# Last bank of a down projection summed in two column halves, and the final norm's gain multiplied in before the rows' factor

## The chip, the cores and the metric

The kernel runs on one core of one Trainium2 chip. The metric is the time of one execution in device microseconds; three runs of the kernel before give 1261.11, 1261.15 and 1261.88 us, a median of 1261.15 us.

The engines are named as the profile names them: PE multiplies matrices and PEld loads its weights, DVE is the vector engine, ACT the scalar engine, POOL the general-purpose engine, SP the queue that issues nearly all transfers. Each works through its own queue in the order written.

## What is computed

One decoder layer on 256 tokens of width 2048: three kinds of self-attention, a cross-attention to a memory, and a gated feed-forward block with 5632 inner columns, each added to x. At the end stands a root-mean-square norm over each token's 2048 values. The change touches only the last two lines:

```python
x = x + conv_glu_ffn(rms_norm(x, g_ffn[l]), w_up[l], conv_w[l], conv_b[l], w_down[l])
return rms_norm(x, g_final)

def rms_norm(x, g):
    y = x * rsqrt(mean(x * x, axis=-1) + NORM_EPS)
    return y * g
```

Everything is float32.

## The kernel before

The tokens are two groups of 128, t = 0 and t = 1. The weights stream through PE in pieces of 128 x 2048 floats; every piece is split by ACT into a high part `hi` (L141) and by DVE into the rest `lo` (L148), and three matmuls (high x high, high x low, low x high) make one float32 product. A list by hand, `before(i, ...)` and `after(i, ...)`, sets where the other work stands between the pieces; no scheduler moves anything, so the order of the code is the order on each engine.

The down projection takes 44 pieces, k = 0 to 43, of 128 rows of `w_down` each. Its result is 256 tokens by 2048 columns: for each t four blocks of 512 columns, n = 0 to 3, each in a PSUM bank of its own, so all eight banks are held (`outs[t, n]`). The first 42 pieces are multiplied into all banks in turn. The last two pieces (`TAIL = 2`) are held back, and then finished bank by bank: for t = 0 the banks n = 0 to 3, then for t = 1 the same, six matmuls of 512 columns each (`down_mm`, L852 to L854).

As soon as a bank is complete, its share of the final norm follows:

- DVE adds the bank to the residual x (L891), which lies in SBUF as `xT`.
- ACT squares the sum and adds up each token's squares into one column of `ss` (`square_sum`, L266); a small ACT instruction, ACTIVATION_READ_ACCUMULATOR, hands the sum out.
- DVE multiplies some blocks by the final gain `gfin` into the output tile `og` (L899); `og` takes a buffer of the pool `raw` and carries that name in the profile.
- After the fourth bank three small DVE instructions (L900 to L902) make mean square plus epsilon, and POOL raises it to the power -0.5 (L904): the factor `r` of each token.
- `finish(n, t, og, r)` scales a block by r and issues its transfer to `out` from SP (L867). For t = 0 the four blocks have their gain already, and are scaled by ACT (n = 0 and 1), DVE (n = 2) and POOL (n = 3) while t = 1 is being computed; DVE's part stands between two adds of t = 1. For t = 1 the blocks 0 and 2 have their gain in `og` and are scaled by ACT; the blocks 1 and 3 take gain and factor in one DVE instruction (L862).

The small sums for t = 1 (L900, over the first three columns of `ss`) stand behind the last add on DVE.

## Time and profile before

| | |
|---|---|
| median of three runs | 1261.15 us |
| the profiled execution's own time | 1260.96 us |
| its span, first to last instruction | 1259.2 us |
| PE busy | 1243.1 us, 99% of the span |
| DVE busy | 831.4 us, 66% |
| ACT busy | 630.3 us, 50% |
| POOL busy | 12.2 us |
| last matmul begins | 1249.80 us after the span's start |
| factor of t = 1 begins on POOL | 1252.14 us |
| last four output transfers are issued from | 1253.49 us |

The profile is one execution of the program on the chip. A line of its timeline gives the start in us from the span's start, the duration, the engine, the line of the kernel, the operation, output and inputs with their shapes, and in square brackets how long the engine had been idle before it and what released it. A DVE instruction may start up to 0.1 us before the one ahead of it ends, since they are pipelined.

### The profile page before, as it was taken

What the parts mean: (1) busy time and instruction counts of PE and PEld (TensorE: products, weight loads), DVE (VectorE), ACT (ScalarE), POOL (GpSimd) and SP (SyncE); (2) the same over time, 40 slices, a digit from 0 to 9 for tenths busy, and PEclk for the clock granted to TensorE, in tenths of its full rate; (3) what the DMA queues carried; (4) which work ended last, traced back from release to release, by engine and by line L of the source; (5) the groups of instructions that cost most, each with busy time, mean ns of one, the idle gap of its engine ahead of it and who ended that gap; (6) DMA issues with size and microseconds to landing.
All of it is one profiled execution on the core that took longest, in us unless ns stands there. A gap on an engine that the chain in (4) does not pass through costs nothing.

```text
span 1259.2 us, 17608 instructions
## 1 busy us (share of the span) xinstructions
PE 1243.1 (99%) x6928; PEld 1078.2 (86%) x6928; DVE 831.4 (66%) x1350; ACT 630.3 (50%) x979; POOL 12.2 (1%) x22
## 2 busy tenths in 40 slices
PE   7999999999999999999999999999999999999997
PEld 6888888988888899888888888888888888888885
DVE  5755677566568877776667768767676754544555
ACT  6545555556455656545444444444444544444444
POOL 0000000000000000000000000000000000000000
PEclk9999999999999999999999999999999999999999
DMA  8755554554566544565565565555656555555541
GB/s 301 236 176 188 186 167 162 181 183 159 174 223 215 170 167 162 202 203 171 167 200 182 186 197 174 183 199 184 198 170 201 186 183 200 181 187 200 175 160 67
DMA packets 104835, 233.23 MB, mean 185 GB/s; under 512 B 4336, under 2 KB 14896, under 8 KB 98992
## 3 DMA queue, kind: packets, MB, share of 16 engines
q1 hardware_dynamic: 104576, 232.05, 55.2%
q8 instruction: 54, 0.88, 0.3%
q14 instruction: 29, 0.24, 0.1%
q10 hardware_dynamic: 144, 0.03, 0.0%
q0 software_dynamic: 32, 0.02, 0.0%
HBM read 229.97 MB, written 2.12 MB: 184 GB/s over the span
## 4 chain that ended last, share of the span: by engine, by line
issue 58%; PE 39%; DMA 2%; DVE 0%; POOL 0%; ACT 0%; SPq 0%; DVEq 0%; POOLq 0%; ACTq 0%
PE acc L296 16%; PE acc L303 9%; PE acc L342 3%; PE acc L344 3%; PE acc L343 3%; DMA raw<-in_w_in 2%; PE at L402 1%; PE acc L299 1%; PE acc L298 1%; PE at L421 0%; PE at L445 0%; PE at L473 0%; PE at L474 0%; ACT hi L141 0%; POOL raw L866 0%
## 5 line engine op out<-in xcount | busy, mean ns | idle before, releaser
L148 DVE TENSOR_TENSOR lo<-raw,hi 128x1024 fp32r<-128x1024 f32 x423 | 517.1, 1223 | 368.1 <-ACT hi L141 367.5
L141 ACT CAST hi<-raw 128x1024 fp32r<-128x1024 f32 x423 | 442.9, 1048 | 480.6 <-PE acc L296 281.0
L296 PE MATMUL acc<-hT,hi 128*128 128x512 f32 x1776 | 631.3, 396 | 4.7 <-ACT hi L141 4.7
L303 PE MATMUL acc<-hT,lo 128*128 128x256 f32 x1840 | 517.7, 283 | 0.9 <-DVE lo L148 0.9
L296 PEld LDWEIGHTS acc<-hT,hi 128*128 128x128 f32 x1776 | 334.0, 188 | 82.0 <-ACT hi L141 5.3
L303 PEld LDWEIGHTS acc<-hT,lo 128*128 128x128 f32 x1840 | 345.6, 188 | 1.6 <-DVE lo L148 1.3
L296 PE MATMUL at<-hT,hi 128*128 128x512 f32 x528 | 189.6, 394 | 0.0
L303 PE MATMUL at<-hT,lo 128*128 128x256 f32 x528 | 149.3, 283 | 0.0
L296 PEld LDWEIGHTS at<-hT,hi 128*128 128x128 f32 x528 | 99.2, 188 | 22.8
L303 PEld LDWEIGHTS at<-hT,lo 128*128 128x128 f32 x528 | 99.3, 188 | 0.0
L854 PE MATMUL acc<-hi,al 128*128 128x512 f32 x220 | 86.8, 395 | 0.0
L853 PE MATMUL acc<-lo,ah 128*128 128x512 f32 x220 | 86.8, 395 | 0.0
L852 PE MATMUL acc<-hi,ah 128*128 128x512 f32 x220 | 86.8, 395 | 0.0
L342 PE MATMUL acc<-hi,hT 128*128 128x256 f32 (+1 forms) x224 | 74.8, 334 | 0.0
L344 PE MATMUL acc<-hi,hT 128*128 128x256 f32 (+1 forms) x224 | 74.0, 330 | 0.0
L343 PE MATMUL acc<-lo,hT 128*128 128x256 f32 (+1 forms) x224 | 73.9, 330 | 0.0
L852 PE MATMUL at<-hi,ah 128*128 128x512 f32 x132 | 52.1, 395 | 0.0
L854 PE MATMUL at<-hi,al 128*128 128x512 f32 x132 | 52.1, 395 | 0.0
L853 PE MATMUL at<-lo,ah 128*128 128x512 f32 x132 | 52.1, 394 | 0.0
L789 ACT ACTIVATE y<-y 128x256 f32<-128x256 f32 x44 | 18.4, 419 | 66.4 <-DVE y L785 66.4
L852 PEld LDWEIGHTS acc<-hi,ah 128*128 128x128 f32 x220 | 41.5, 188 | 9.7
L853 PEld LDWEIGHTS acc<-lo,ah 128*128 128x128 f32 x220 | 41.5, 188 | 9.7
(157 smaller groups left out, 1004.2 us busy)
## 6 DMA issues: line engine op xcount, KB each, us to landing
raw<-in_w_up SPq DMA_DIRECT2D x88, 1024.0 KB, 5.1
raw<-in_w_in SPq DMA_DIRECT2D x45, 1024.0 KB, 5.3
raw<-in_w_down SPq DMA_DIRECT2D x44, 1024.0 KB, 4.9
raw<-in_w_out SPq DMA_DIRECT2D x12, 1024.0 KB, 5.3
raw<-in_w_ckv SPq DMA_DIRECT2D x8, 1024.0 KB, 5.6
raw<-in_w_out SPq DMA_DIRECT2D x8, 512.0 KB, 5.0
raw<-in_w_cq SPq DMA_DIRECT2D x4, 1024.0 KB, 5.4
raw<-in_w_co SPq DMA_DIRECT2D x4, 1024.0 KB, 5.3
```

Of the source, the lines that this page charges most:

```text
L141: ACT.copy(hi, p.raw[:, h * HALF:(h + 1) * HALF])
L148: DVE.tensor_tensor(lo, p.raw[:, h * HALF:(h + 1) * HALF], hi.bitcast(F32), op=ALU.subtract)
L296: PE.matmul(accs[n], w, x, start=(i == 0), stop=False)
L298: PE.matmul(accs[n][:, :S], w, x[:, :S], start=(i == 0), stop=False)
L303: PE.matmul(accs[n][:, :S], lo[:, j, n * P:(n + 1) * P], src()[:, korder[i], :S], start=False, stop=(i == len(korder) - 1))
L342: PE.matmul(o, xh, hi[:, j, :], start=(i == 0), stop=False)
L343: PE.matmul(o, xh, lo[:, j, :], start=False, stop=False)
L344: PE.matmul(o, xl, hi[:, j, :], start=False, stop=(i == len(korder) - 1))
L789: after(cur[0] + 1 + n, lambda: ACT.activation(gate[k], gate[k], AF.Silu))
L852: PE.matmul(o, ah, wh, start=(k == 0), stop=False)
L853: PE.matmul(o, ah, wl, start=False, stop=False)
L854: PE.matmul(o, al, wh, start=False, stop=(k == KF - 1))
```

## The change

Only the end of the down projection, `finish` and the size of `ss3` are edited.

- For t = 1 the bank n = 3 is finished in two halves. The last two pieces are first multiplied into columns 0 to 255 of the bank, with six matmuls of 256 columns; then into columns 256 to 511, with six more, but into a bank of their own (`own`), which is started afresh and holds only the last two pieces' part. When the first half is done, DVE adds the whole bank, 512 columns, to x (its right half still lacks the last two pieces), and when the second is done, 256 columns of `own`.
- The squares of t = 1 come in five columns, the last two of 256 values each. The small sums over the first four (L896, L897) stand on DVE ahead of the add of the second half; only the last small instruction (L912) is behind it.
- Each block of t = 1 is multiplied by the gain as soon as it is added, as for t = 0, so DVE has four such multiplications for t = 1 (the last in two halves) where it had two.
- The scalings by r are dealt out anew. t = 0: ACT has n = 0 and 1, POOL n = 2 and 3, DVE none; they are issued in the order 2, 0, 3, 1. t = 1: DVE has n = 0 and 2, now a plain multiplication by r, ACT n = 1 and 3.
- `ss3` has 10 columns for 8.

```diff
-    def down_mm(p, k, h, t, n):
+    def down_mm(p, k, h, t, n, c0=0, c1=512, own=None):
         hi, lo = p.parts[h]
         ah, al = (a[:, t * P:(t + 1) * P] for a in parts[k])
-        o = outs[t, 2 * h + n]
-        wh, wl = hi[:, n * 512:(n + 1) * 512], lo[:, n * 512:(n + 1) * 512]
-        PE.matmul(o, ah, wh, start=(k == 0), stop=False)
+        o, first = (outs[t, 2 * h + n][:, c0:c1], 0) if own is None else (own, KF - TAIL)
+        wh, wl = (a[:, n * 512 + c0:n * 512 + c1] for a in (hi, lo))
+        PE.matmul(o, ah, wh, start=(k == first), stop=False)
...
     def finish(n, t, og, r):
         col = slice(n * 512, (n + 1) * 512)
-        if t and n % 2:
-            DVE.scalar_tensor_tensor(og[:, col], xtok(t, n), r, gfin["t"][:, col], op0=ALU.mult, op1=ALU.mult)
-        elif t or n < 2:
+        if t:
+            if n % 2:
+                ACT.activation(og[:, col], og[:, col], AF.Copy, scale=r)
+            else:
+                DVE.tensor_scalar_mul(og[:, col], og[:, col], r)
+        elif n < 2:
             ACT.activation(og[:, col], og[:, col], AF.Copy, scale=r)
         else:
-            (DVE, POOL)[n - 2].tensor_scalar_mul(og[:, col], og[:, col], r)
+            POOL.tensor_scalar_mul(og[:, col], og[:, col], r)
...
-                    ss = ss3[:, 4 * t:4 * t + 4]
-                    for n in range(4):
+                    ss = ss3[:, 5 * t:5 * t + 5]
+
+                    parts_of = ((0, 0, 512), (1, 0, 512), (2, 0, 512)) + (((3, 0, 256), (3, 256, 512)) if t else ((3, 0, 512),))
+                    for i, (n, c0, c1) in enumerate(parts_of):
+                        own = any_tile()[:, :c1 - c0] if c0 else None
                         for kk in range(KF - TAIL, KF):
-                            down_mm(fin[kk], kk, n // 2, t, n % 2)
-                        col = slice(n * 512, (n + 1) * 512)
-                        xc = xtok(t, n)
-                        DVE.tensor_tensor(xc, outs[t, n], xc, op=ALU.add)
-                        square_sum(xc, ss[:, n:n + 1])
+                            down_mm(fin[kk], kk, n // 2, t, n % 2, c0, c1, own)
+                        if t and i == len(parts_of) - 1:
+                            DVE.reduce_sum(ms[:, 0:1], ss[:, :i], axis=AX.X)
+                            DVE.tensor_scalar(ms[:, 0:1], ms[:, 0:1], 1.0 / D, EPS, op0=ALU.mult, op1=ALU.add)
+                        xc = xtok(t, n)[:, c0:c1]
+                        if own is None:
+                            DVE.tensor_tensor(xtok(t, n), outs[t, n], xtok(t, n), op=ALU.add)
+                        else:
+                            DVE.tensor_tensor(xc, own, xc, op=ALU.add)
+                        square_sum(xc, ss[:, i:i + 1], c1 - c0)
                         if done:
-                            for m in ((3, 0, 1), (2,), (), ())[n]:
+                            for m in ((2, 0), (3, 1), (), (), ())[i]:
                                 finish(m, *done)
-                        gains = ((), (0,), (), (2,)) if t else ((0,), (1,), (2,), (3,))
-                        for m in gains[n]:
-                            col = slice(m * 512, (m + 1) * 512)
-                            DVE.tensor_tensor(og[:, col], xtok(t, m), gfin["t"][:, col], op=ALU.mult)
-                    DVE.reduce_sum(ms[:, 0:1], ss[:, :3], axis=AX.X)
-                    DVE.tensor_scalar(ms[:, 0:1], ms[:, 0:1], 1.0 / D, EPS, op0=ALU.mult, op1=ALU.add)
-                    DVE.scalar_tensor_tensor(ms[:, 1:2], ss[:, 3:4], 1.0 / D, ms[:, 0:1], op0=ALU.mult, op1=ALU.add)
+                        col = slice(n * 512 + c0, n * 512 + c1)
+                        DVE.tensor_tensor(og[:, col], xc, gfin["t"][:, col], op=ALU.mult)
+                    if not t:
+                        DVE.reduce_sum(ms[:, 0:1], ss[:, :3], axis=AX.X)
+                        DVE.tensor_scalar(ms[:, 0:1], ms[:, 0:1], 1.0 / D, EPS, op0=ALU.mult, op1=ALU.add)
+                    DVE.scalar_tensor_tensor(ms[:, 1:2], ss[:, i:i + 1], 1.0 / D, ms[:, 0:1], op0=ALU.mult, op1=ALU.add)
```

This is how DVE's queue ends in the kernel before, from the first add of t = 1 on (`xT` is x, `raw` the output tile, `msf` and `ss_96` the small sums; the bracket names the engine whose count is waited for):

```order
L891 TENSOR_TENSOR xT<-at,xT 128x512 [waits PE_49] x2
L866 TENSOR_SCALAR raw<-raw,rfin 128x512 [waits Pool_49]
L899 TENSOR_TENSOR raw<-xT,gfin 128x512 [waits DVE_49]
L891 TENSOR_TENSOR xT<-at,xT 128x512 [waits PE_49]
L891 TENSOR_TENSOR xT<-acc,xT 128x512 [waits PE_49]
L899 TENSOR_TENSOR raw<-xT,gfin 128x512 [waits DVE_49]
L900 TENSOR_REDUCE msf<-ss_96 128x1 [waits Activation_49]
L901 TENSOR_SCALAR msf<-msf 128x1 [waits DVE_49]
L902 SCALAR_TENSOR_TENSOR msf<-ss_96,msf 128x1 [waits DVE_49,Activation_49]
L862 SCALAR_TENSOR_TENSOR raw<-xT,rfin,gfin 128x512 [waits Pool_49]
L862 SCALAR_TENSOR_TENSOR raw<-xT,rfin,gfin 128x512
```

Only two of the four adds have a gain multiplication behind them here, each some instructions after its add, and DVE scales one block of t = 0 in between.

And this is its end in the changed kernel, from the second add of t = 1 on (one add and one gain multiplication of t = 1 stand ahead of it):

```order
L900 TENSOR_TENSOR xT<-at,xT 128x512 [waits PE_49]
L908 TENSOR_TENSOR raw<-xT,gfin 128x512 [waits DVE_49]
L900 TENSOR_TENSOR xT<-at,xT 128x512 [waits PE_49]
L908 TENSOR_TENSOR raw<-xT,gfin 128x512 [waits DVE_49]
L900 TENSOR_TENSOR xT<-acc,xT 128x512 [waits PE_49]
L908 TENSOR_TENSOR raw<-xT,gfin 128x256 [waits DVE_49]
L896 TENSOR_REDUCE msf<-ss_96 128x1 [waits Activation_49]
L897 TENSOR_SCALAR msf<-msf 128x1 [waits DVE_49]
L902 TENSOR_TENSOR xT<-acc,xT 128x256 [waits PE_49]
L908 TENSOR_TENSOR raw<-xT,gfin 128x256 [waits DVE_49]
L912 SCALAR_TENSOR_TENSOR msf<-ss_96,msf 128x1 [waits Activation_49]
L865 TENSOR_SCALAR raw<-raw,rfin 128x512 [waits Pool_49]
```

Each add of t = 1 is now followed by a gain multiplication that waits for it; the sum over `ss` and its wait for ACT, which stood behind the last add, stand ahead of it.

ACT's queue at the same place, as one piece of the difference between the two (its first row is the four squares of t = 0 and the first of t = 1):

```order
 L266 ACTIVATE junk,ss_96<-xT 128x512 x5
-L864 ACTIVATE raw<-raw,rfin 128x512 x2
-L266 ACTIVATE junk,ss_96<-xT 128x512 x3
-L864 ACTIVATE raw<-raw,rfin 128x512 x2
-L1059 UNCONDITIONAL_BRANCH
+L867 ACTIVATE raw<-raw,rfin 128x512
+L266 ACTIVATE junk,ss_96<-xT 128x512
+L867 ACTIVATE raw<-raw,rfin 128x512
+L266 ACTIVATE junk,ss_96<-xT 128x512
+L266 ACTIVATE junk,ss_96<-xT 128x256 x2
+L863 ACTIVATE raw<-raw,rfin 128x512 x2
+L1069 UNCONDITIONAL_BRANCH
```

The two scalings of t = 0 are drawn apart by a square of t = 1, and the last square has become two of half the width.

## Rows read from the trace of the kernel before

**Rows 1.** The page's first part: busy time, share of the span and count of instructions of each engine.

```profile
PE 1243.1 (99%) x6928; PEld 1078.2 (86%) x6928; DVE 831.4 (66%) x1350; ACT 630.3 (50%) x979; POOL 12.2 (1%) x22
```

**Rows 2.** The timeline, PE alone: the first and the last of the six matmuls of the last bank.

```profile
1248.64 0.39 PE L852 MATMUL acc<-hi,ah 128*128 128x512 f32 x1
...
1249.80 0.40 PE L854 MATMUL acc<-hi,al 128*128 128x512 f32 x1
```

**Rows 3.** The timeline, DVE alone: the first adds of t = 0, and everything from the small sums of t = 0 on.

```profile
1240.47 0.69 DVE L891 TENSOR_TENSOR xT<-acc,xT 128x512 f32<-128x512 f32 x1 [1.88 <-PE acc L854]
1241.20 0.69 DVE L899 TENSOR_TENSOR raw<-xT,gfin 128x512 f32<-128x512 f32 x1
1241.87 0.69 DVE L891 TENSOR_TENSOR xT<-acc,xT 128x512 f32<-128x512 f32 x1
...
1245.99 0.15 DVE L900 TENSOR_REDUCE msf<-ss 128x1 f32<-128x3 f32 x1
1246.18 0.15 DVE L901 TENSOR_SCALAR msf<-msf 128x1 f32<-128x1 f32 x1
1246.44 0.16 DVE L902 SCALAR_TENSOR_TENSOR msf<-ss,msf 128x1 f32<-128x1 f32 x1
1246.52 0.68 DVE L891 TENSOR_TENSOR xT<-at,xT 128x512 f32<-128x512 f32 x1
1247.44 0.69 DVE L891 TENSOR_TENSOR xT<-at,xT 128x512 f32<-128x512 f32 x1 [0.24 <-PE at L854]
1248.05 0.48 DVE L866 TENSOR_SCALAR raw<-raw,rfin 128x512 f32<-128x512 f32 x1
1248.44 0.68 DVE L899 TENSOR_TENSOR raw<-xT,gfin 128x512 f32<-128x512 f32 x1
1249.04 0.68 DVE L891 TENSOR_TENSOR xT<-at,xT 128x512 f32<-128x512 f32 x1
1250.24 0.69 DVE L891 TENSOR_TENSOR xT<-acc,xT 128x512 f32<-128x512 f32 x1 [0.51 <-PE acc L854]
1250.85 0.68 DVE L899 TENSOR_TENSOR raw<-xT,gfin 128x512 f32<-128x512 f32 x1
1251.44 0.15 DVE L900 TENSOR_REDUCE msf<-ss 128x1 f32<-128x3 f32 x1
1251.63 0.15 DVE L901 TENSOR_SCALAR msf<-msf 128x1 f32<-128x1 f32 x1
1251.89 0.16 DVE L902 SCALAR_TENSOR_TENSOR msf<-ss,msf 128x1 f32<-128x1 f32 x1
1252.74 1.41 DVE L862 SCALAR_TENSOR_TENSOR raw<-xT,rfin,gfin 128x512 f32<-128x512 f32 x2 [0.69 <-POOL rfin L904]
```

**Rows 4.** The timeline, ACT alone: the squares and scalings that lie beside the adds of t = 1.

```profile
1247.30 0.63 ACT L266 ACTIVATE junk<-xT 128x512 bf16<-128x512 f32 x1 [1.13 <-DVE xT L891]
...
1247.93 1.32 ACT L864 ACTIVATE raw<-raw,rfin 128x512 f32<-128x512 f32 x2
1249.15 0.61 ACT L266 ACTIVATE junk<-xT 128x512 bf16<-128x512 f32 x1
...
1251.02 0.63 ACT L266 ACTIVATE junk<-xT 128x512 bf16<-128x512 f32 x1 [0.41 <-DVE xT L891]
1251.56 0.19 ACT L266 ACTIVATION_READ_ACCUMULATOR junk<-xT 128x1 f32 x1
1252.74 1.33 ACT L864 ACTIVATE raw<-raw,rfin 128x512 f32<-128x512 f32 x2 [1.00 <-POOL rfin L904]
```

**Rows 5.** The timeline, POOL alone, from the factor of t = 0 on.

```profile
1246.68 0.55 POOL L904 TENSOR_TENSOR rfin<-msf,mhalf 128x1 f32<-128x1 f32 x1 [728.06 <-DVE msf L902]
1247.33 1.66 POOL L866 TENSOR_SCALAR raw<-raw,rfin 128x512 f32<-128x512 f32 x1
1252.14 0.57 POOL L904 TENSOR_TENSOR rfin<-msf,mhalf 128x1 f32<-128x1 f32 x1 [3.15 <-DVE msf L902]
```

**Rows 6.** SP's issues of the last four output transfers, from the timeline.

```profile
1253.49 1.80 SPq L867 DMA_DIRECT2D out<-raw  x4
```

**Rows 7.** The view of stretches of half a us where the data of these transfers begins and where it ends; its columns are the stretch, its length, busy time of PE, PEld, DVE, ACT and POOL with their instructions, the granted clock, the share of the DMA engines and GB/s.

```profile
1254.00:1254.50 0.50, 0.00 (x0) 0.00 (x0) 0.16 (x1) 0.07 (x1) 0.00 (x0) 0.75 0.36 135
...
1257.00:1257.50 0.50, 0.00 (x0) 0.00 (x0) 0.00 (x0) 0.00 (x0) 0.00 (x0) 0.50 0.35 127
```

**Rows 8.** The timeline at 478 us, PE alone: two neighbours in a row of matmuls of 256 columns with a change of weights at each.

```profile
478.20 0.28 PE L342 MATMUL acc<-hi,hT 128*128 128x256 f32 x1
...
478.32 0.28 PE L343 MATMUL acc<-lo,hT 128*128 128x256 f32 x1
```

**Rows 9.** The groups of instructions by line and shape: DVE's float32 add of 128 x 256 out of PSUM into x; behind the bar the busy time, the mean ns of one and the idle time before them.

```profile
L674 DVE TENSOR_TENSOR xT<-acc,xT 128x256 f32<-128x256 f32 x32 | 12.4, 419 | 0.5
```

**Rows 10.** The timeline, ACT alone, in the attention: a square of 128 columns with a sum, and the reading of that sum.

```profile
136.01 0.27 ACT L266 ACTIVATE junk<-at 128x128 bf16<-128x128 f32 x1
136.18 0.19 ACT L266 ACTIVATION_READ_ACCUMULATOR junk<-at 128x1 f32 x1
```

**Rows 11.** The timeline, ACT and DVE, in the attention: an exponential of 256 columns with a sum, the reading of that sum, and the DVE instruction that waits for it.

```profile
122.55 0.50 ACT L439 ACTIVATE s<-s,nm 128x256 f32<-128x256 f32 x1
...
122.95 0.19 ACT L439 ACTIVATION_READ_ACCUMULATOR s<-s,nm 128x1 f32 x1
...
123.17 0.18 DVE L505 RECIPROCAL r<-l 128x4 f32<-128x4 f32 x1
```

More of the change, by code (lines that the diff above doesn't have):

```diff
@@ L845, in a_low @@
         DVE.tensor_tensor(lo, ffn["a"][:, k, :], hi.bitcast(F32), op=ALU.subtract)
-    def down_mm(p, k, h, t, n):
+    def down_mm(p, k, h, t, n, c0=0, c1=512, own=None):
         hi, lo = p.parts[h]
         ah, al = (a[:, t * P:(t + 1) * P] for a in parts[k])
-        o = outs[t, 2 * h + n]
-        wh, wl = hi[:, n * 512:(n + 1) * 512], lo[:, n * 512:(n + 1) * 512]
-        PE.matmul(o, ah, wh, start=(k == 0), stop=False)
+        o, first = (outs[t, 2 * h + n][:, c0:c1], 0) if own is None else (own, KF - TAIL)
+        wh, wl = (a[:, n * 512 + c0:n * 512 + c1] for a in (hi, lo))
+        PE.matmul(o, ah, wh, start=(k == first), stop=False)
         PE.matmul(o, ah, wl, start=False, stop=False)
         PE.matmul(o, al, wh, start=False, stop=(k == KF - 1))
-    ss3 = small(8, "ss3", 1)
+    ss3 = small(10, "ss3", 1)
     fin = {}
```

## The prediction

> **What bounds the kernel now.** I read the page's first part, then the timeline of each engine over the last 20 us. The page says that PE is busy for 99% of the span [rows 1]: until the last matmul only PE counts, and the change gives PE the same columns to multiply. So everything is decided behind PE, in the last 10 us of 1259. There the reader is to see one string of small steps. The last matmul ends at 1249.80 + 0.40 = 1250.20 [rows 2]; DVE adds the bank at 1250.24 [rows 3]; ACT squares it from 1251.02 and reads the sum from 1251.56 to 1251.75 [rows 4]; DVE's small sums end with L902 at 1251.89 [rows 3]; POOL makes the factor from 1252.14 to 1252.71 [rows 5]; DVE and ACT scale from 1252.74 [rows 3, 4]; SP issues from 1253.49 [rows 6]; the data flows from about 1254.3 to 1257.2 [rows 7]. Four issues take 1.80 us while their data takes some 2.9, so the transfers start with the first issue and then run at their own rate: the end moves as the first issue moves. From the last matmul to the factor are 1.94 us, and the change wants to shorten this.
>
> **PE.** Six matmuls of 512 columns become twelve of 256. Neighbours of 256 columns, each with new weights, start 0.12 us apart [rows 8]; those of 512 start (1249.80 - 1248.64) / 5 = 0.232 apart [rows 2]. Twelve take 1.42 us for 1.39: nothing. The first half is done at about 1248.64 + 5 x 0.12 + 0.28 = 1249.52, the second at 1250.2 as now.
>
> **DVE up to the last full add.** This is the term that decides. Rules from rows 3: an instruction that doesn't wait for the one ahead starts about 0.60 us after an operation of 512 columns (1248.44 to 1249.04, 1250.24 to 1250.85); a gain that waits for its own add starts 0.73 after it (1240.47 to 1241.20). In t = 0 a pair of add and gain takes 1.40 (1240.47 to 1241.87), and PE delivers a bank every 6 x 0.232 = 1.39, so that pair is PE's pace; DVE's own would be 0.73 + 0.60 = 1.33. Hence DVE can keep up with PE but hardly catch up. And it starts t = 1 late: the small sums of t = 0 put the first add at 1246.52, though that bank, three before the last, had been complete 0.5 us earlier (1250.20 - 3 x 1.39 = 1246.03). Before, DVE caught up, since for three adds it had one gain and one scaling of 0.48 between them, and it even waited 0.51 for the last bank [rows 3]. Now it has three full pairs: adds at 1246.52, 1247.85, 1249.18 and the last full one at 1246.52 + 3 x 1.33 = 1250.51, 1.0 us after its half bank is ready and 0.27 later than the last add starts today. The early start that the halving should give is lost in DVE's queue.
>
> **From there to the factor.** The small sums over four columns now stand ahead of the second half's add and wait for ACT, so a wait is added, and queued behind it on DVE are that add, its gain and the last small sum; ACT, POOL and SP wait for those. Step by step:
> - the first half's square starts 0.78 after the add began (1250.24 to 1251.02 [rows 3, 4]): 1251.29. ACT is free by then: its squares of 0.63 and two scalings of 0.66 fit between DVE's adds [rows 4].
> - a square of 256 columns from SBUF isn't in the trace. From its start to the reading of the sum are 0.54 for 512 columns [rows 4], 0.17 for 128 [rows 10], 0.40 for an exponential of 256 [rows 11]. I take 0.31, on the line between the two squares, which is the same operation; 0.2 and 0.4 are the ends. Reading takes 0.19: 1251.79.
> - DVE's sum follows 0.03 behind a reading (123.14 to 123.17 [rows 11]); 0.14 is the other end (1251.75 to 1251.89). 1251.82; the next small one 0.19 later, the second half's add 0.08 behind that (as 1246.44 to 1246.52 [rows 3]): 1252.09. PE has been done for 1.9 us.
> - that add takes 0.42 [rows 9], the square starts 0.09 behind it (0.78 less 0.69), then again 0.31 + 0.19 + 0.03: the last small sum at 1253.13. The half gain lies beside the square and costs nothing.
> - the factor starts 0.25 later (1251.89 to 1252.14 [rows 3, 5]): 1253.38, which is **1.24 us later than now**.
>
> **Behind the factor.** The first block of t = 1 is now scaled by DVE with a plain multiplication, 0.48 [rows 3], where its issue came 1253.49 - 1252.74 = 0.75 after the start of the scalings. With 0.04 for the issue that gives 0.52: **0.23 gained**. The second DVE block and ACT's two (1.33 in all [rows 4]) are ready before the transfers ahead of them have flowed. The third of four issues of t = 0 now waits for POOL's second scaling, at 1247.33 + 2 x 1.66 = 1250.65 [rows 5], and the fourth behind it; their data is through some 2 us before that of t = 1 starts, and POOL is free 2.7 us before the new factor. Hidden; without that cover each us of delay on POOL would count in full.
>
> **Sum.** +1.24 - 0.23 = +1.0 us. The profiled execution, 1260.96 with a span of 1259.2, becomes 1261.96; it stands 0.19 below the median of 1261.15, so the median becomes **1262.15**. The bounds: three pairs at 1.20 (two waitless steps) or at 1.40 give -0.4 or +0.2; two squares of 256, -0.2 or +0.2; two hand-overs from ACT, 0 or +0.2. The likeliest case's own range is 1261.5 to 1262.8, and the scatter of the three runs, up to 0.7 above the median, is to be added above.
>
> **The rivals.**
> - *DVE keeps PE's pace.* If the last full add came at 1249.55, right behind its half bank, every step would be 0.96 earlier: the factor at 1252.42, still 0.28 late, since the wait for the first half's square stands ahead of the second half's add; less 0.23, the time is 1261.2. For it: the pair's own pace is my inference, no row shows DVE catching up on pairs. Against: 1.0 us would have to be caught up in three pairs. Chance 0.10.
> - *The change does what it is written for.* The second half is added when PE ends, at 1250.24, squared from 1250.75, the factor starts at about 1251.6, 0.5 early, and with the 0.23 the time is 1260.4. It needs DVE on PE's pace and the sums over ACT's first half ready before 1250.2. Against: add, square and reading of the first half alone take 0.78 + 0.31 + 0.19 = 1.28 from 1249.55. Chance 0.03.
> - *Slower by more: DVE's gains and POOL's scalings get in each other's way.* Today one POOL scaling, 1247.33 to 1248.99, lies beside DVE; now two, up to 1250.65, lie beside the gains of t = 1. In rows 3 a gain, which reads two operands from SBUF, started at 1248.44 inside POOL's span and took 0.68 as always, 0.39 behind the instruction ahead: no stop. But POOL's span is rough, and its access may have been over. If a gain had to wait for the scaling that runs, the second gain (due 1248.58) would start at 1248.99, +0.4; if the next scaling went first, at 1250.65, +2.07, and the time would be 1264.2. It decides from 1.5 us of such waiting on: then the change is measurably slower. Chance 0.06.
>
> The Trainium skill, on the page "SBUF — State Buffer", section "SBUF: two separate sides", speaks for that last rival: the port pair that DVE and GpSimd share is "an exclusive lock, not a bandwidth split", also for a DVE operation with two SBUF inputs against a GpSimd one that reads SBUF, and whoever starts first holds it for the whole instruction. By that rule the gain at 1248.44 should have stood until 1248.99; the trace does not show it, unless POOL's row is longer than its access.
>
> The last 0.03 is for what the trace can't show, such as the tiles that move because `ss3` grows.
>
> **How the numbers follow.** Forecast 0.78, DVE on PE's pace 0.10, the gain as written 0.03, POOL and DVE in each other's way 0.06, others 0.03. A measurement of this kernel tells about 0.2%, 2.5 us, from no change, so the forecast and the first two rivals all count as no change: same 0.93. Slower by more needs the third rival with most of its price: 0.05. Faster has only unseen causes: 0.02. The range 1261.1 to 1263.2 holds nearly all of the forecast with the scatter of runs above it, and the first rival at 1261.2.
>
> **What would show it.** In the changed kernel's timeline: the last full add on DVE near 1250.5 with no idle time ahead of it, while its matmuls end near 1249.5; L896 with idle time before it that ACT ended, near 1251.8; the second half's add near 1252.1; the factor near 1253.4; SP's last issues from about 1254.5. If DVE's gains start late behind POOL's row, the third rival holds; if L896 shows no wait for ACT, my string is wrong; if the last full add is at 1249.6, the first rival. PE's end elsewhere than 1250.2 would mean that I am wrong about the matmuls.

## The result, and the profile after

The changed kernel takes 1254.38 us (median of six runs, 1253.29 to 1255.44) beside 1261.38 us for the kernel before (six runs, 1261.11 to 1261.88): a ratio of 0.9948 with a 95% interval of 0.9938 to 0.9959. It is 7.0 us faster, where 1262.15 was forecast and a range that began at 1261.1. The profiled execution took 1254.24 us, with a span of 1252.5.

The end of the program looks as forecast. The timeline of DVE alone, with the first add of t = 1 and then from the third on (L900 is now the full add, L902 that of the second half, L908 the gain; answers to [rows 3]):

```profile
1238.81 0.68 DVE L900 TENSOR_TENSOR xT<-at,xT 128x512 f32<-128x512 f32 x1
...
1241.46 0.68 DVE L900 TENSOR_TENSOR xT<-at,xT 128x512 f32<-128x512 f32 x1
1242.18 0.70 DVE L908 TENSOR_TENSOR raw<-xT,gfin 128x512 f32<-128x512 f32 x1
1242.80 0.68 DVE L900 TENSOR_TENSOR xT<-acc,xT 128x512 f32<-128x512 f32 x1
1243.51 0.42 DVE L908 TENSOR_TENSOR raw<-xT,gfin 128x256 f32<-128x256 f32 x1
1244.11 0.16 DVE L896 TENSOR_REDUCE msf<-ss 128x1 f32<-128x4 f32 x1 [0.17 <-ACT junk L266]
1244.30 0.15 DVE L897 TENSOR_SCALAR msf<-msf 128x1 f32<-128x1 f32 x1
1244.37 0.41 DVE L902 TENSOR_TENSOR xT<-acc,xT 128x256 f32<-128x256 f32 x1
1244.82 0.42 DVE L908 TENSOR_TENSOR raw<-xT,gfin 128x256 f32<-128x256 f32 x1
1245.42 0.16 DVE L912 SCALAR_TENSOR_TENSOR msf<-ss,msf 128x1 f32<-128x1 f32 x1 [0.18 <-ACT junk L266]
1246.27 0.88 DVE L865 TENSOR_SCALAR raw<-raw,rfin 128x512 f32<-128x512 f32 x2 [0.69 <-POOL rfin L914]
```

ACT's two squares of half the width, POOL alone, the first and the last matmul of the last bank, and SP's last issues (four timelines of the changed kernel, for [rows 4], [rows 5], [rows 2] and [rows 6]):

```profile
1243.57 0.42 ACT L266 ACTIVATE junk<-xT 128x256 bf16<-128x256 f32 x1 [0.61 <-DVE xT L900]
1243.89 0.18 ACT L266 ACTIVATION_READ_ACCUMULATOR junk<-xT 128x1 f32 x1
```

```profile
1238.97 0.55 POOL L914 TENSOR_TENSOR rfin<-msf,mhalf 128x1 f32<-128x1 f32 x1 [722.95 <-DVE msf L912]
1239.62 3.59 POOL L869 TENSOR_SCALAR raw<-raw,rfin 128x512 f32<-128x512 f32 x2
1245.66 0.57 POOL L914 TENSOR_TENSOR rfin<-msf,mhalf 128x1 f32<-128x1 f32 x1 [2.46 <-DVE msf L912]
```

```profile
1240.95 0.28 PE L852 MATMUL acc<-hi,ah 128*128 128x256 f32 x1
...
1242.27 0.28 PE L854 MATMUL acc<-hi,al 128*128 128x256 f32 x1
```

```profile
1246.79 1.80 SPq L870 DMA_DIRECT2D out<-raw  x4
```

The reader is to see two things. Counted from the end of the last matmul, everything behind it is later: 1242.27 + 0.28 = 1242.55 is that end now, the factor starts 3.11 us after it for 1.94 before, the issues 4.24 for 3.29, and the span ends 9.92 us after it for 8.98. That is the loss of 1.0 us that was forecast. But the last matmul itself ends at 1242.55, where it ended at 1250.20: PE came to the end of its work 7.65 us sooner. -7.65 + 0.94 = -6.71 us, and the spans differ by 1252.5 - 1259.2 = -6.7.

Most of this is not a wait that has gone: in the long stretches PE has no gap in either kernel, and yet it runs faster. The view of stretches for PE alone (length, busy time with the count of matmuls in the bracket, granted clock, share of the DMA engines, GB/s), first of the kernel before, then of the changed one; 600 to 900 us lies in the up projection, 1050 to 1200 in the down projection:

```profile
600.00:900.00 300.00, 300.00 (x1716) 1.00 0.56 186
1050.00:1200.00 150.00, 150.00 (x647) 1.00 0.55 189
```

```profile
600.00:900.00 300.00, 300.00 (x1739) 1.00 0.57 187
1050.00:1200.00 150.00, 150.00 (x645) 1.00 0.55 186
```

The granted clock is 1.00 (2.4 GHz) in all four. In 300 us of the up projection PE does 1739 matmuls for 1716, 1.3% more; in the down projection 2 fewer of 647. All traces here record the same 6928 matmuls in the same order (up to the last bank, where the halves make it twelve for six), so a stretch can be timed from one matmul's start to another's: 2860 matmuls of the up projection (504.0 to 1002.5 us in the kernel before) take 498.5 us before and 492.5 after, 1040 of the down projection (1002.5 to 1243.5) take 241.0 and 241.9. In the up projection, from start to start, the median from an L296 to the L303 behind it falls from 233 to 229 ns and from that to the next L296 from 120 to 117. These two stretches stand in the experiments as **up** and **down**.

The first 504 us are another matter. They are 2.6 us shorter (501.4), but 1.9 of these are less idle time of PE while the kernel starts. The first 100 us, in the view of [rows 7] with its columns, before and after, with the same 492 matmuls:

```profile
0.00:100.00 100.00, 92.91 (x492) 79.38 (x493) 61.37 (x89) 51.49 (x72) 2.14 (x10) 0.98 0.69 236
```

```profile
0.00:100.00 100.00, 94.80 (x492) 81.11 (x493) 61.61 (x89) 51.58 (x72) 2.14 (x10) 0.97 0.70 236
```

Over all traces of this case, PE's idle time ahead of the 504 us lies between 4.9 and 7.5 us and follows no distance of tiles, so 1.9 us of the 7.65 is scatter of the two profiled executions. In **up** and **down** PE is never idle.

### The profile page after: what moved, and what is told of

Its sections match the earlier page's. It is cut to its first block, busy times and chain, and to the rows that moved or that the text cites. A ratio compares the mean times of both kernels' runs of the same rounds, so it can differ in the third digit from the quotient of the medians.

```text
span 1252.5 us, 17626 instructions
## 1 busy us (share of the span) xinstructions
PE 1237.3 (99%) x6934; PEld 1074.2 (86%) x6934; DVE 832.0 (66%) x1353; ACT 630.3 (50%) x981; POOL 14.2 (1%) x23
## 4 chain that ended last, share of the span: by engine, by line
issue 58%; PE 37%; DMA 2%; DVE 2%; POOL 0%; ACT 0%; SPq 0%; ACTq 0%; POOLq 0%; DVEq 0%
PE acc L296 16%; PE acc L303 8%; PE acc L342 3%; PE acc L343 3%; PE acc L344 3%; DMA raw<-in_w_in 2%; PE at L402 1%; DVE lo L148 1%; PE at L421 0%; PE at L445 0%; DVE hT L198 0%; PE acc L298 0%; PE acc L299 0%; PE at L473 0%; POOL raw L869 0%
## 5 line engine op out<-in xcount | busy, mean ns | idle before, releaser
L296 PE MATMUL acc<-hT,hi 128*128 128x512 f32 x1776 | 626.3, 395 | 2.8 <-ACT hi L141 2.8
L303 PE MATMUL acc<-hT,lo 128*128 128x256 f32 x1840 | 512.5, 280 | 0.9 <-DVE lo L148 0.9
L296 PEld LDWEIGHTS acc<-hT,hi 128*128 128x128 f32 x1776 | 334.9, 189 | 77.5 <-ACT hi L141 3.4
L303 PEld LDWEIGHTS acc<-hT,lo 128*128 128x128 f32 x1840 | 345.7, 189 | 1.7 <-DVE lo L148 1.4
L296 PE MATMUL at<-hT,hi 128*128 128x512 f32 x528 | 187.5, 392 | 0.0
L303 PE MATMUL at<-hT,lo 128*128 128x256 f32 x528 | 147.6, 280 | 0.0
L296 PEld LDWEIGHTS at<-hT,hi 128*128 128x128 f32 x528 | 99.1, 188 | 21.8
L303 PEld LDWEIGHTS at<-hT,lo 128*128 128x128 f32 x528 | 99.2, 188 | 0.0
L852 PE MATMUL acc<-hi,ah 128*128 128x512 f32 (+1 forms) x222 | 88.1, 397 | 0.0
L854 PE MATMUL acc<-hi,al 128*128 128x512 f32 (+1 forms) x222 | 87.0, 392 | 0.0
L853 PE MATMUL acc<-lo,ah 128*128 128x512 f32 (+1 forms) x222 | 86.6, 390 | 0.0
L852 PE MATMUL at<-hi,ah 128*128 128x512 f32 x132 | 52.7, 399 | 0.0
L854 PE MATMUL at<-hi,al 128*128 128x512 f32 x132 | 52.0, 394 | 0.0
L853 PE MATMUL at<-lo,ah 128*128 128x512 f32 x132 | 51.7, 392 | 0.0
L854 PEld LDWEIGHTS acc<-hi,al 128*128 128x128 f32 x222 | 41.7, 188 | 10.7
L853 PEld LDWEIGHTS acc<-lo,ah 128*128 128x128 f32 x222 | 41.7, 188 | 9.7
```

What stands on the lines that cost most here:

```text
L296: PE.matmul(accs[n], w, x, start=(i == 0), stop=False)
L303: PE.matmul(accs[n][:, :S], lo[:, j, n * P:(n + 1) * P], src()[:, korder[i], :S], start=False, stop=(i == len(korder) - 1))
L852: PE.matmul(o, ah, wh, start=(k == first), stop=False)
L853: PE.matmul(o, ah, wl, start=False, stop=False)
L854: PE.matmul(o, al, wh, start=False, stop=(k == KF - 1))
```

## The experiments

The edit of the end can't reach back 700 us. One thing in the diff can: `ss3` has 10 columns for 8. A tile of 8 floats takes 32 bytes of each partition, one of 10 takes 64, so all tiles that are allocated after `ss3` begin 32 bytes further: the four large activations `hT` among them, which stream through PE in the up projection, and `ah` and `al`, the weights of the down projection. The pieces' `hi` and `lo`, which are the weights of the up projection and stream in the down projection, stay. In the built programs `hT` begins at byte 117600 before and at 117632 after.

**Theory A**: the place of these tiles sets PE's pace. **Theory B**: the edit of the tail brings the time by itself.

**a1_pad32: the tiles moved, the tail untouched.**

```diff
-    ss3 = small(8, "ss3", 1)
+    ss3 = small(10, "ss3", 1)
```

> The kernel before with one edit: ss3 has 10 columns for 8 (two are never used), so every tile allocated after it, hT, ah and al among them, lies 32 bytes further, as in the changed kernel. Theory A (the time came from where hT lies: it now begins at a multiple of 64 bytes): in the trace the matmuls of L296 and L303 start 230 and 117 ns apart as in the changed kernel, for 233 and 120, and the time is the changed kernel's without its 1.0 us of a slower tail, about 1253.4. Theory B (the edit of the tail itself brings the time): no change, 1261.4.

Measured: 1253.18 us (four runs), ratio 0.9937 (0.9922 to 0.9952) against runs of the kernel before made beside it; up 492.5, down 241.9; the span ends 8.96 us behind the last matmul. Its windows are those of the changed kernel to one matmul:

```profile
600.00:900.00 300.00, 300.00 (x1739) 1.00 0.55 188
1050.00:1200.00 150.00, 150.00 (x644) 1.00 0.55 189
```

**a2_edit_only: the changed kernel with its tiles put back.**

```diff
-    ss3 = small(10, "ss3", 1)
+    ss3 = small(8, "ss3", 1)
...
-                    ss = ss3[:, 5 * t:5 * t + 5]
+                    ss = ss3[:, 4 * t:4 * t + 4]
+                    fifth = ffn["p"].tile([P, 1], F32, name="fifth") if t else None
...
-                        square_sum(xc, ss[:, i:i + 1], c1 - c0)
+                        square_sum(xc, ss[:, i:i + 1] if i < 4 else fifth, c1 - c0)
...
-                    DVE.scalar_tensor_tensor(ms[:, 1:2], ss[:, i:i + 1], 1.0 / D, ms[:, 0:1], op0=ALU.mult, op1=ALU.add)
+                    DVE.scalar_tensor_tensor(ms[:, 1:2], ss[:, i:i + 1] if i < 4 else fifth, 1.0 / D, ms[:, 0:1], op0=ALU.mult, op1=ALU.add)
```

> The changed kernel with its tiles put back: ss3 has 8 columns again, and the fifth sum of t = 1 has a tile of its own that is allocated last, so hT, ah and al lie where they lay before. Theory A: the slower tail alone, the prediction's +1.0: 1262.4, with the factor of t = 1 about 1.2 us later against the last matmul. Theory B: as the changed kernel, 1254.4.

Measured: 1262.45 us (ten runs), ratio 1.0012 (1.0003 to 1.0021); up 498.5, down 241.0; the factor starts 3.14 us behind the last matmul, the span ends 9.96 behind it. In its windows, with all engines as in [rows 7], PE's counts are those of the kernel before to one matmul:

```profile
600.00:900.00 300.00, 300.00 (x1717) 263.17 (x1716) 211.40 (x319) 138.50 (x189) 0.00 (x0) 1.00 0.54 186
1050.00:1200.00 150.00, 150.00 (x647) 121.64 (x646) 75.18 (x81) 64.88 (x81) 0.00 (x0) 1.00 0.55 190
```

Theory B has fallen: the edit alone costs time, and the two unused columns alone bring about 8 us.

**a3_pad64 and a4_cst32: how far, and against what?** a3 gives `ss3` 24 columns. a4 leaves `ss3` and puts an unused tile ahead of everything:

```diff
+    pad = cst.tile([P, 8], F32, name="pad")
+    POOL.memset(pad, 0.0)
     gT = cst.tile([P, 4 * KD + 1], F32, name="gT")
```

> The kernel before with ss3 of 24 columns: the tiles behind it move by 64 bytes, so hT begins 32 bytes off a multiple of 64 again. Theory A, if the multiple of 64 counts: as before, 1261.4. Its rival A2 (any move of these tiles, or their distance to other tiles, does it): near 1253. Theory B: 1261.4.

> The kernel before with an unused tile of 32 bytes ahead of all others: all tiles, hi, lo, hT, ah and al, move from 32 bytes off to a multiple of 64. Theory A, if the start of the operand that streams through PE counts: hT as in the changed kernel, and in the down projection, where hi and lo stream, the 1056 matmuls gain about 3 ns each too (3 us): near 1250. Rival A3 (what counts is that the streaming operand and the weights begin at different offsets from a multiple of 64): all offsets are equal again, so as before, 1261.4.

Measured: a3 1260.01 us (ten runs), ratio 0.9992 (0.9983 to 1.0002), but with up 501.7 and down 237.4: slower in one stage, faster in the other, as its windows show:

```profile
600.00:900.00 300.00, 300.00 (x1706) 1.00 0.54 185
1050.00:1200.00 150.00, 150.00 (x657) 1.00 0.56 190
```

a4 1260.23 us (ten runs), ratio 0.9994 (0.9984 to 1.0003), up 498.5 and down 241.0, just as in the kernel before, though `hi`, `lo`, `hT`, `ah` and `al` now all begin at multiples of 64. The windows of a4 have the very counts of the kernel before:

```profile
600.00:900.00 300.00, 300.00 (x1716) 1.00 0.54 185
1050.00:1200.00 150.00, 150.00 (x647) 1.00 0.55 189
```

So the multiple of 64 in theory A was wrong, and A3 stands in so far as it isn't where a tile lies that counts, but how far tiles lie from each other.

**b1 to b4, c1 and c2: the distance in steps.** The same one-line edit with 32, 40, 56, 72, 48 and 64 columns.

> The kernel before with hT, ah and al 96 bytes further from hi and lo than they were (ss3 of 32 columns). The runs so far gave, for a distance changed by 0, 32 and 64 bytes, 498.5, 492.5 and 501.7 us for the same stretch of the up projection (hT streams, hi and lo are the weights) and 241.0, 241.9 and 237.4 us for the same stretch of the down projection (hi and lo stream, ah and al are the weights); moving all tiles together changed neither. Theory A3 (the distance between the streaming tile and the weights' tile decides): a third pair of values, or one of these. If the pattern repeats after 64 bytes: 492.5 and 241.9; but then 64 should have been as 0. Rival A4 (something else that moves with them, such as the small tiles): no prediction of the two stretches.

> The kernel before with hT, ah and al 128 bytes further from hi and lo (ss3 of 40 columns). If the pattern repeats after 128 bytes: as in the kernel before, 498.5 us for the stretch of the up projection and 241.0 us for that of the down projection. If its period is longer: other values.

> The kernel before with hT, ah and al 192 bytes further from hi and lo (ss3 of 56 columns). If the pattern repeats after 128 bytes: as with 64, 501.7 and 237.4 us. If after 256: possibly as the distance of 64 the other way, another pair.

> The kernel before with hT, ah and al 256 bytes further from hi and lo (ss3 of 72 columns). If the pattern repeats after 128 or 256 bytes: as in the kernel before, 498.5 and 241.0 us, and about 1261. If its period is longer: other values.

> The kernel before with hT, ah and al 160 bytes further from hi and lo (ss3 of 48 columns). 256 bytes gave the very values of 0 (498.49 and 240.99 us), so by theory A3 the pattern has a period of 256 bytes, and 160 is one of its eight steps of 32 that has not been seen: some pair between those seen, 492 to 502 us for the stretch of the up projection and 235 to 242 for that of the down projection.

> The kernel before with hT, ah and al 224 bytes further from hi and lo (ss3 of 64 columns): the last of the eight steps, again a pair between those seen.

Measured, with the runs above (the times without a count are one run each; the kernel before, run beside the experiments, had medians of 1260.57 to 1261.44, beside b1 to b4 one run of 1260.59):

| bytes further | up, us | down, us | time, us |
|---|---|---|---|
| 0 (before) | 498.5 | 241.0 | 1261.38 (6) |
| 32 (a1) | 492.5 | 241.9 | 1253.18 (4) |
| 64 (a3) | 501.7 | 237.4 | 1260.01 (10) |
| 96 (b1) | 501.5 | 242.0 | 1265.97 |
| 128 (b2) | 493.1 | 235.1 | 1247.76 |
| 160 (c1) | 492.5 | 241.9 | 1252.16 |
| 192 (b3) | 497.0 | 242.0 | 1260.29 |
| 224 (c2) | 497.1 | 243.0 | 1261.45 |
| 256 (b4) | 498.5 | 241.0 | 1262.62 |

At 256 bytes the values of 0 come back, so the pattern seems to repeat after 256 bytes, of which this one distance is the test, and it doesn't after 128 (128 is not as 0, nor 192 as 64). The windows of b4:

```profile
600.00:900.00 300.00, 300.00 (x1717) 1.00 0.56 186
1050.00:1200.00 150.00, 150.00 (x647) 1.00 0.55 189
```

The up projection differs by 1.9% between its best and its worst distance, the down projection by 3.3%, and the distances that are good for one aren't always good for the other: 32 and 160 bytes are best for the up projection only, 128 is good for both.

One rival can be settled from the traces: that ACT and DVE, which split the next pieces meanwhile, get in PE's way more at some distances. The mean step from L852 to L853 is 237.7 ns in a1 and 225.8 ns in a3, where ACT is at work during the whole step and DVE not at all (81 steps) just as where DVE is and ACT is not (126 steps). So their work beside PE isn't what the distance changes; the transfers, which run all the time, are not ruled out by this.

**c3_two_pads: each stage at a good distance of its own.**

```diff
     buf0 = ctx.enter_context(tc.tile_pool(name="buf0", bufs=1))
+    POOL.memset(buf0.tile([P, 8], F32, name="pad0"), 0.0)
...
         ffn["a"] = f.tile([P, KF, S], F32, name="a")
+        POOL.memset(f.tile([P, 24], F32, name="pad1"), 0.0)
```

> The kernel before, its tail and its small tiles untouched, with two unused tiles: 32 bytes ahead of hT and 96 more ahead of ah and al, so that hT lies 32 and ah and al 128 bytes further from hi and lo than before. Theory A3: each stage takes the value of its own distance: 492.5 us for the stretch of the up projection, 235.1 for that of the down projection, and the time is the 1253.2 of 32 bytes alone less 241.9 - 235.1 = 6.8, about 1246.4. Rival A4 (the small tiles that moved too, or one distance for all): 492.5 or 235.1 not reached, 1253 or more.

Measured: 1246.68 us (four runs), ratio 0.9883 (0.9866 to 0.9899); up 492.4, down 235.1. Its windows:

```profile
600.00:900.00 300.00, 300.00 (x1738) 1.00 0.57 186
1050.00:1200.00 150.00, 150.00 (x663) 1.00 0.57 192
```

A4 has fallen, since the small tiles stayed where they were; each stage goes by its own distance, `hT` from the pieces in the one and `ah` and `al` from them in the other.

**c4_sums_behind: the step of the tail that decided.** In the changed kernel the lines of L896 and L897 move behind the second half's add:

```diff
-                        if t and i == len(parts_of) - 1:
-                            DVE.reduce_sum(ms[:, 0:1], ss[:, :i], axis=AX.X)
-                            DVE.tensor_scalar(ms[:, 0:1], ms[:, 0:1], 1.0 / D, EPS, op0=ALU.mult, op1=ALU.add)
...
                         square_sum(xc, ss[:, i:i + 1], c1 - c0)
+                        if t and i == len(parts_of) - 1:
+                            DVE.reduce_sum(ms[:, 0:1], ss[:, :i], axis=AX.X)
+                            DVE.tensor_scalar(ms[:, 0:1], ms[:, 0:1], 1.0 / D, EPS, op0=ALU.mult, op1=ALU.add)
```

> The changed kernel, its tiles where they are, with the two small sums over the first four columns moved behind the second half's add on DVE. The prediction's chain: the add no longer stands behind the wait for ACT, begins 0.34 us behind the half gain, some 0.5 us earlier than now, and the factor of t = 1 begins about 7.9 us after the first add of t = 1 ... that is 6.85 - 0.5 = 6.35 us after it (1238.81 to 1245.66 in the changed kernel). Rival (DVE's queue alone sets the time, or ACT's second square is late for another reason): the factor stays 6.85 us after the first add.

Measured: the factor starts 6.34 us after the first add of t = 1 (1238.63 to 1244.97) and 2.61 us behind the last matmul, for 3.11; the span ends 9.41 us behind it, for 9.92 in the changed kernel; 1253.58 us in one run. The second half's add on DVE and the factor on POOL in c4:

```profile
1243.68 0.42 DVE L899 TENSOR_TENSOR xT<-acc,xT 128x256 f32<-128x256 f32 x1
```

```profile
1244.97 0.57 POOL L914 TENSOR_TENSOR rfin<-msf,mhalf 128x1 f32<-128x1 f32 x1 [1.95 <-DVE msf L912]
```

The wait ahead of the add had cost 0.5 us. The tail is still 0.4 us longer than that of the kernel before.

**d1_tail_two_pads and d3_gain_ahead: can the halves gain?** d1 takes the distances of c3, the halves and the sums behind, and deals gains and scalings out as in the kernel before; the last gain of t = 1 stands beside POOL's factor. d3 moves that gain ahead of the sums. The difference between d1 and d3:

```diff
-                        if t and i == len(parts_of) - 1:
-                            DVE.reduce_sum(ms[:, 0:1], ss[:, :i], axis=AX.X)
-                            DVE.tensor_scalar(ms[:, 0:1], ms[:, 0:1], 1.0 / D, EPS, op0=ALU.mult, op1=ALU.add)
...
-                        for m in ((), (0,), (), (), ())[i] if t else (i,):
+                        for m in ((), (0,), (), (), (2,))[i] if t else (i,):
                             gain(m)
+                        if t and i == len(parts_of) - 1:
+                            DVE.reduce_sum(ms[:, 0:1], ss[:, :i], axis=AX.X)
+                            DVE.tensor_scalar(ms[:, 0:1], ms[:, 0:1], 1.0 / D, EPS, op0=ALU.mult, op1=ALU.add)
...
-                    if t:
-                        gain(2)
                     r = small(1, "rfin")
```

> The tiles of c3 (hT 32 and ah and al 128 bytes further), with a third tail: the last bank of t = 1 in two halves as in the changed kernel, but the small sums behind the second half's add, and the gains and scalings dealt out as in the kernel before (two gain multiplications of t = 1, the second behind the last small sum, beside POOL's factor). If DVE's queue was what ate the gain of the halves: the second half's add begins within 0.2 us of the end of its matmuls, the factor of t = 1 begins about 1.5 us after the last matmul's end, where the kernel before has 1.94 and the changed one 3.2, and the time is some 0.4 us under c3's 1246.7, 1246.3, too little for the median to show. If halving itself costs as much as it saves: 1.9 us or more.

> d1 with its last gain multiplication of t = 1 moved from beside POOL's factor to ahead of the small sums, where DVE stood idle for 0.6 us. In d1 the factor took 0.95 us instead of 0.57, and ended 0.44 us behind that gain. If the gain, which reads two operands from SBUF, holds POOL up: the factor takes 0.57 us again, starts about 1.9 us after the last matmul's end and ends at about 2.45, and the span's end lies 8.9 us behind the last matmul, for 9.27 in d1 and 8.97 in c3. If the 0.95 us had another cause (POOL itself, or where the factor lies): 0.95 again and 9.27.

Measured: d1 1246.37 us (four runs), ratio 0.9891 (0.9874 to 0.9907); the second half's add begins 0.24 us behind its matmuls, the factor starts 1.84 behind them where 1.5 was expected, and takes 0.95. PE's last matmul, DVE's add of the second half and its last gain, and POOL's factor in d1:

```profile
1234.99 0.28 PE L855 MATMUL acc<-hi,al 128*128 128x256 f32 x1
```

```profile
1235.51 0.42 DVE L901 TENSOR_TENSOR xT<-acc,xT 128x256 f32<-128x256 f32 x1
...
1236.95 0.68 DVE L890 TENSOR_TENSOR raw<-xT,gfin 128x512 f32<-128x512 f32 x1
```

```profile
1237.12 0.95 POOL L918 TENSOR_TENSOR rfin<-msf,mhalf 128x1 f32<-128x1 f32 x1 [3.05 <-DVE msf L914]
```

and DVE's last gain, ACT's last squares and POOL's factor in d3:

```profile
1236.08 0.68 DVE L890 TENSOR_TENSOR raw<-xT,gfin 128x512 f32<-128x512 f32 x1
```

```profile
1235.26 0.63 ACT L266 ACTIVATE junk<-xT 128x512 bf16<-128x512 f32 x1
...
1236.01 0.42 ACT L266 ACTIVATE junk<-xT 128x256 bf16<-128x256 f32 x1
...
1236.55 0.42 ACT L266 ACTIVATE junk<-xT 128x256 bf16<-128x256 f32 x1
1236.88 0.19 ACT L266 ACTIVATION_READ_ACCUMULATOR junk<-xT 128x1 f32 x1
```

```profile
1237.37 0.57 POOL L916 TENSOR_TENSOR rfin<-msf,mhalf 128x1 f32<-128x1 f32 x1 [3.07 <-DVE msf L914]
```

d3 takes 1245.93 us (four runs), ratio 0.9876 (0.9859 to 0.9892), the lowest median here; the factor takes 0.57, ends 2.45 us behind the last matmul, and the span ends 8.92 behind it, for 9.27 in d1 and 8.96 in c3. So the gain beside it had held the factor up by 0.38 us. And even at its best the halving brings nothing that can be told from none, since the kernels with the tail of before end 8.96 to 9.00 behind their last matmul: ACT now sets the end of the string, with three squares in a row behind its scalings of t = 0 (in d3 from 1235.26 to 1237.07). That d3's median is 0.75 below c3's is no more than their scatter (1245.17 to 1247.14 for c3).

**d2_lo128 and d4_hi128: what collides?** An unused tile of 128 bytes between `hi` and `lo` in d2, ahead of `hi` and ahead of `lo` in d4, the rest moved by 256 (in d2 with `ss3` of 40 columns as well):

```diff
+    POOL.memset(wpool.tile([P, 32], F32, name="pad2"), 0.0)
```

> The kernel before with lo alone moved by 128 bytes against hi, and hT, ah and al by 256, which by the runs so far is as if they had not moved. If what counts is the tile that streams in one matmul against the weights that are loaded meanwhile for the next: in the down projection lo streams only in the middle one of three matmuls, so only the step from L853's start to L854's falls from 232 ns to about 226, the other two stay near 232, and the stretch of the down projection takes 241.0 - 1040 / 3 x 5.6 ns = 239.0 us; in the up projection every second weight load is lo's, and the stretch lies between 493.1 and 498.5, about 496. If the tiles as a whole or the engines that write hi and lo (ACT, DVE) were what counts: both stretches as before, 498.5 and 241.0, or as with 128 bytes, 493.1 and 235.1.

> The counterpart of d2_lo128: the kernel before with hi alone moved by 128 bytes, lo, hT, ah and al by 256, which is as if they had not moved. d2 gave 232.5, 225.8 and 228.3 ns for the three steps of the down projection (L852 to L853, L853 to L854, L854 to L852), where all were 232.2 to 232.6; the middle one is that in which lo streams. If the streaming tile against the weights loaded meanwhile decides: the first and the last step, in which hi streams, fall to about 226, and the middle one stays near 232; the stretch takes some 237.1 us. If hi has no part in it: 232 in all three and 241.0 us.

Measured: d2 up 499.8, down 237.4, 1259.18 us in one run; the three steps of the down projection (L852 to L853, L853 to L854, L854 to the next L852) 232, 226 and 228 ns. d4 up 497.0, down 242.0, 1257.21 us in one run; the steps 236, 234 and 230. The rule that each step follows the tile that streams in it got the first two steps of d2 right and little else: its third step, expected near 232, fell to 228, the two steps of d4 that should have fallen to 226 took 236 and 230, and the up projection of d2, expected at 496, became slower than before. It falls as stated. a1 speaks against it too: there `hi` streams in L852 and in L854, equally far from both weight tiles if multiples of 256 bytes don't count, and yet the three steps take 238, 231 and 232 ns. Nor do the tiles count as a whole, by which both stretches would be as before or as at 128 bytes: neither d2 nor d4 is so. What meets what is not settled.

## Why the prediction was wrong

- **PE: "the change gives PE the same columns to multiply", so the last matmul ends where it ended.** This is the step that failed. The columns are the same, but not their addresses: PE's end moved by -7.65 us, of which -6.07 lie in the stretch of the up projection, +0.95 in that of the down projection, +0.05 behind them and -2.58 in the 504 us ahead of them, where `hT` streams too but where 1.9 us are less idle time, which the tiles don't explain. a1 and a2 show it from both sides: two unused columns alone give 1253.18, the edit without them 1262.45. The prediction's own sign of being wrong, PE's end elsewhere than 1250.2, came true, though not by the two sizes of matmul that it had in mind. The 3 in 100 kept for "the tiles that move because `ss3` grows" was the right place with no price; the rows could not give one, since one trace has one distance.
- **The two sizes of matmul** cost next to nothing, as forecast: twelve take 1242.55 - 1240.95 = 1.60 us from the first start to the last end, six took 1250.20 - 1248.64 = 1.56.
- **DVE up to the last full add**: right. The adds of t = 1 came 1.33 us apart, without idle time (1241.46 to 1242.80, 1.34).
- **From there to the factor**: right. L896 waited for ACT, ACT's half square takes 0.32 to its reading where 0.31 was taken (the line between the two squares, redone, gives 0.17 + 0.37 x 128/384 = 0.29, so that this term came out so near is in part luck), and from the first add of t = 1 to the factor are 6.85 us (1238.81 to 1245.66), where 1253.38 - 1246.52 = 6.86 was forecast. c4 confirms the wait's part by taking it away: 0.5 us.
- **Behind the factor**: right within 0.01. From the factor's end to the first issue are 0.56 us (1246.23 to 1246.79) for 0.78 before, 0.22 gained.
- **The sum for the tail**, +1.0 us: 0.94 in the trace, and a2, which has the edit alone, is slower than the runs beside it by a ratio of 1.0012 (1.0003 to 1.0021), 0.4 to 2.6 us; its median of 1262.45 is near the forecast of 1262.15.
- **The rivals**: DVE did not keep PE's pace, and the change did not do what it was written for. Gains and scalings beside each other did not delay DVE: the gain at 1242.18 lies inside POOL's row and DVE's steps kept their 1.33. It is POOL that is slower: its two scalings took 3.59 us, 1.80 each, for 1.66 and 1.59 where fewer gains lay beside them (that the gains are the cause is not shown), and d1's factor took 0.95 for 0.57. In the changed kernel that cover was long enough.

By the rule that the Trainium skill gives for the port pair of DVE and POOL (page "SBUF — State Buffer", section "SBUF: two separate sides"), whoever starts first holds the pair and the other blocks. d1 and d3 agree for POOL behind a DVE operation with two SBUF inputs: the factor that starts 0.17 us behind the gain takes 0.95, and 0.57 where no gain runs. DVE behind a running POOL scaling shows no such stop in any trace here: the gain at 1242.18 took 0.70, in POOL's row of 1239.62 to 1243.21.

## What to carry to other kernels

In a kernel whose PE is busy for 99% of the span, a tile that grows by a few bytes can weigh more than the work that was edited, here about 8 us against 1: look at the addresses of everything that is allocated behind an edit, and when a change is to be judged, time the untouched stages by the same matmuls first, and keep the idle time of the start out of it. An edit and its side effect are told apart by two kernels, the side effect alone and the edit without it. Halving the last step of a chain gains only if every engine of the chain is free to start early; here DVE's queue, then a wait put ahead of work that was ready, then ACT, each in turn took it back.

## What the runs showed of the hardware

**PE's pace depends on how far apart in SBUF the tiles that its matmuls read lie.** With float32 tiles of 128 partitions and PE at a granted clock of 1.00 (2.4 GHz), moving the activations' tiles (`hT`, `ah`, `al`) against those of the pieces (`hi`, `lo`) by steps of 32 bytes changed the pace of the up projection between 492.5 and 501.7 us for 2860 matmuls and that of the down projection between 235.1 and 243.0 us for 1040 (226 to 234 ns each); 256 bytes gave the values of 0 again, 128 did not, and moving all five together by 32 bytes changed nothing. It repeats to 0.1 us from trace to trace (six kernels with `hT` 32 bytes further: 492.4 to 492.5), on three chips, and isn't seen in any wait: PE counts as busy throughout.

The Trainium skill, page "TensorE: Matmul & The Clock Gate", section "Part 2: What happens when you issue a matmul", says of PE's two read ports that "Loading the next tile's weights doesn't steal SBUF read bandwidth from the running matmul". The runs neither bear that out nor refute it: they show that PE's pace is not independent of where the other tile lies, and leave open whether it is the loading of weights that meets the streaming operand; a1, d2 and d4 speak against the simplest form of that.

**POOL is slowed by DVE beside it**: a factor of 128 x 1 takes 0.55 to 0.57 us, and 0.95 in d1, where a DVE multiplication of two SBUF tiles runs beside its start; moved away from it, in d3, 0.57 again.
